# Weight operands of the first feed-forward projection off their 32-byte edges

## The chip, the cores and the metric

The kernel runs on one core of a Trainium2 chip. The metric is the device time of one execution in microseconds (us), the median over the runs.

## The reference

One layer of an encoder over 2048 tokens with 1024 features, in float32: windowed attention (16 query heads, 4 key and value heads, 128 tokens to each side, a bias by distance and a learned sink), then a SwiGLU feed-forward network with 2816 hidden features. Each sub-layer has a norm before and after it and is scaled, shifted and gated by a vector c. The part that the change touches is the first projection of the feed-forward network:

```python
def swiglu(h, w_in, w_out):
    a, b = jnp.split(h @ w_in, 2, axis=-1)
    return (jax.nn.silu(a) * b) @ w_out
...
        h = rmsnorm(x, ffn_norm_pre[i]) * (1.0 + sc2) + sh2
        y = swiglu(h, ffn_w_in[i], ffn_w_out[i])
        x = x + g2 * rmsnorm(y, ffn_norm_post[i])
```

## The kernel before

**Stages.** The tokens go in four chunks of 512. The projections to queries, keys and values, the attention in blocks of 128 queries, and the output projection (tiles `ol` and `wo`) come first and are interleaved; they fill some 700 us. Then come the two feed-forward projections, each in two halves of 1024 tokens.

**Precision.** Every float32 operand is held as two tiles of a rounded type: a high part, made by a cast on ScalarE, and a low part, the difference of value and high part, made by a subtraction on VectorE (`split`). A product takes three matmuls (`three`): high by high, high by low, low by high. The first factor of each is the stationary one, which TensorE loads (LDWEIGHTS) before each matmul; the second one streams through in 512 columns.

**The feed-forward projections.** A `Block` is a product of 2 by 2 blocks by Strassen's method in Winograd's form: seven products in place of eight. It loads two column tiles of weights (`wiri`), makes four sums and differences of their quarters on VectorE (`s1` to `s4`), and splits seven operands `a11`, `s2`, `a12`, `s3`, `s1`, `a22`, `s4` into tiles `w...` of 2 by 4 by 128 words a partition: the high part, then the low part, each with four stationary operands of 128 by 128. In the profile they are named `wa_i` and `ws_i`. Each of the seven products takes 4 times 3 matmuls, and `Hidden.take` adds the results up on VectorE (`p1`, `u2`, `u3`, `b1` as `p_i`, `u_i`, `b_i`); the moving operands are `hb` and `ht`. There are 22 blocks for each half of the tokens. Products of the two halves of SwiGLU and the differences for the second projection are written for GpSimd.

**Places.** The operand tiles of the first projection come from two pools, `wi0` and `wi1`, used in turn by the blocks, each with a tag `w` of 7 places. The second projection (`Outs`) uses the same `Block` with a pool `wo` of 11 places. A place's size is rounded up to 32 bytes, and places stand one behind the other from an address that is a multiple of 32; other tiles of the stage lie behind them in the same memory.

**Order.** A recording layer takes down all operations, gives each tile a place and each engine its order, and only then emits the program, so every instruction has the line of the emitting call (L748). Priorities come from a backward pass, and of 18 rounds the one with the best replay is kept. The planner knows which rows and which pieces of 64 words of a tile an operation touches (`Buf.unit`, `region`), and which earlier tiles lay where a new one comes to lie (`place`). An addition or product that the kernel writes for GpSimd may be given to VectorE (`others`). Transfers are all issued from one queue (SyncE).

One line elsewhere has a part in the prediction: the probabilities of the attention, which are transposed as stationary operands:

```python
            pr = pp.tile([P, GRP, 3 * P + 1], F32, tag="pr", name=f"pr{u}")
...
                    pe.transpose(pt[:, h * P:(h + 1) * P], pr[:, h, jj * P:(jj + 1) * P], ident)
```

With P = 128 and GRP = 4, a head's row is 385 words. The other transposes, of values (`vt`), take blocks of 128 words from rows of 512.

Of the kernel before, what the change touches and what calls it, by code (L numbers as in the profile page):

```python
# [14 lines left out]
F32R = mybir.dt.float32r  # L15
# [5 lines left out]
P = 128  # L21
# [731 lines left out]
def f(ap):  # L753
    return ap.bitcast(F32)
# [8 lines left out]
def encoder_layer(ctx, tc, a):  # L763
# [81 lines left out]
    def split(hi, lo, src, eng):  # L845
        act.copy(hi, src)
        return eng.tensor_tensor(lo, src, f(hi), ALU.subtract)
# [8 lines left out]
    class Chunk:  # L856


        def __init__(self, c):
            self.c, self.hh = c, [None] * KT  # L860
            self.xt = [xs.tile([P, CH], F32, tag="x", name=f"x{c}_{k}") for k in range(KT)]
            for k in range(KT):
                sp.dma_start(self.xt[k], a["xT"][c, :, k, :])
# [524 lines left out]
    wbufs = 7  # L1388
# [6 lines left out]
    class Operands:  # L1395
# [12 lines left out]
        def load(self, *names):  # L1408

            for n in names:  # L1410
                for k in range(self.m):
                    hi, lo = self.slot(n, k)
                    sp.dma_start(f(lo), self.src(n, k))
                    split(hi, lo, f(lo), dve)

    class Block:

        STEPS = tuple(zip(("a11", "s2", "a12", "s3", "s1", "a22", "s4"), OPERANDS))

        def __init__(self, ops, i, u, wa, wb, keep=None, kept=None):  # L1420
            self.ops, self.u, m = ops, u, ops.m
            pl = wi[i % len(wi)]
            if kept:
                self.w = {}
                for n, _ in self.STEPS:
                    self.w[n] = w = pl.tile([P, 2, m, P], F32R, tag="w", bufs=wbufs, name=f"w{n}_{u}")
                    sp.dma_start(f(w), kept[n])
                return
            raw = pl.tile([P, 2, 2 * m, P], F32, tag="raw", name=f"wir{u}")
            sp.dma_start(raw[:, 0], wa)  # L1430
            sp.dma_start(raw[:, 1], wb)
            a11, a12, a21, a22 = [raw[:, i].rearrange("p (k e) c -> p e k c", e=2)[:, e] for i in range(2) for e in range(2)]
            sm_ = {n: pl.tile([P, m, P], F32, tag=n, name=f"{n}_{u}", bufs=1) for n in ("s1", "s2", "s4")}
            sm_["s3"] = a21
            dve.tensor_tensor(sm_["s1"], a21, a22, ALU.add)
            dve.tensor_tensor(sm_["s2"], sm_["s1"], a11, ALU.subtract)
            dve.tensor_tensor(sm_["s3"], a11, a21, ALU.subtract)
            dve.tensor_tensor(sm_["s4"], a12, sm_["s2"], ALU.subtract)
            src = dict(sm_, a11=a11, a12=a12, a22=a22)
            self.w = {}  # L1440
            for n, _ in self.STEPS:
                w = pl.tile([P, 2, m, P], F32R, tag="w", bufs=wbufs, name=f"w{n}_{u}")
                split(w[:, 0], w[:, 1], src[n], dve)
                self.w[n] = w
                if keep:
                    sp.dma_start(keep[n], f(w))
# [155 lines left out]
    wbufs = 11  # L1602
# [120 lines left out]
    t0, m = 2 * FIRST[-1][-1], 2 * PARTS[-1][-1]  # L1723
    gs, wl = {}, []
    for j in range(CPH):
        c = NCH - CPH + j
# [4 lines left out]
    for n in range(KT):  # L1731
        raw = wi[0].tile([P, 2, 2 * MD * P], F32, tag="raw", name=f"wlr{n}").rearrange("p a b -> p (a b)")[:, :m * P]
        sp.dma_start(raw, a["w_out"][n, :, t0:t0 + m].rearrange("p k c -> p (k c)"))
        t = hB.tile([P, 2, CH], F32R, tag=("t1", "t4", "b22")[n // 3], name=f"wl{n}")
# [3 lines left out]
    for i, (c, cols) in enumerate([(NCH - 2, slice(0, CH)), (NCH - 1, slice(0, CH // 2)), (NCH - 1, slice(CH // 2, CH))]):  # L1738
        for n in range(KT):
# [4 lines left out]
            for k in range(m):  # L1744
                w, g = wl[n], gs[c, k]
# [83 lines left out]
```

## Time and profile before

| | |
|---|---|
| median of the runs | 2037.47 us |
| runs | 2036.68 to 2038.26 us (2) |
| profiled execution, its own time | 2036.67 us |
| its span, first to last instruction | 2034.9 us |
| mean granted TensorE clock | 0.995 |

PE is TensorE's matmuls, PEld its weight loads, DVE VectorE, ACT ScalarE, POOL GpSimd, SP the queue that issues transfers. A tile's buffer numbers are left out of its name, so that `ws_i` stands for all operands of the first projection made from a sum or difference. In `bank<-ht,ws_i` the moving operand stands first and the stationary one second. Where durations are given as three numbers, they are the least, the median and the greatest, in ns. What an engine waited for is inferred from semaphores.

### The profile page before, as it was taken

How to read it: one execution, taken by the hardware profiler on the slowest of the kernel's cores; microseconds unless marked ns; L12 is line 12 of the kernel's file. 1: busy time of each engine (PE TensorE's matmuls, PEld its weight loads, DVE VectorE, ACT ScalarE, POOL GpSimd, SP SyncE). 2: the span in 40 equal slices, each digit the busy share in tenths (PEclk: the TensorE clock that was granted, in tenths of full speed). 3: DMA queues.
4: the chain of work that ended last, by engine and by line, in shares of the span. 5: the costliest groups of instructions: out<-in, count | busy, mean ns of one | idle time of the engine just before them, and what ended most of it. 6: DMA issues, size and time to landing. Idle time of an engine off the chain costs nothing.

```text
span 2034.9 us, 28945 instructions
## 1 busy us (share of the span) xinstructions
PE 1991.0 (98%) x9366; PEld 1659.3 (82%) x9366; DVE 1703.6 (84%) x3075; ACT 1069.9 (53%) x2094; POOL 554.4 (27%) x501
## 2 busy tenths in 40 slices
PE   5999999999999999999999999999999999999997
PEld 4888888888787778788888888888888888888886
DVE  7868888877989888988787998776776789989998
ACT  5557766777778864344343533333333744455432
POOL 1302342344657513432333221111111000120031
PEclk9999999999999999999999999999999999999999
DMA  8896765576787694444446743333233694398543
GB/s 308 303 324 211 241 210 173 192 279 229 253 279 251 226 361 150 160 161 166 165 160 242 272 155 130 119 135 104 83 124 105 240 334 144 117 326 297 173 154 109
DMA packets 208580, 415.23 MB, mean 204 GB/s; under 512 B 19963, under 2 KB 61996, under 8 KB 205356
## 3 DMA queue, kind: packets, MB, share of 16 engines
q1 hardware_dynamic: 207852, 412.84, 58.7%
q8 instruction: 75, 1.23, 0.2%
q14 instruction: 77, 0.63, 0.1%
q10 hardware_dynamic: 576, 0.52, 0.1%
HBM read 278.52 MB, written 134.77 MB: 203 GB/s over the span
## 4 chain that ended last, share of the span: by engine, by line
PE 91%; DVE 5%; DMA 2%; issue 1%; ACT 1%; SPq 0%; POOL 0%; DVEq 0%; ACTq 0%; POOLq 0%
PE bank L748 91%; DVE z L748 1%; DVE ada L748 1%; DVE zx L748 1%; DVE pr L748 0%; DMA o_d<-of 0%; DMA ly<-y_d 0%; DMA x<-xT 0%; DMA ol<-o_d 0%; SPq L748 0%; DVE u_i L748 0%; DMA ada<-ada_w 0%; DVE x L748 0%; DVE plo L748 0%; DVE ws_i L748 0%
## 5 line engine op out<-in xcount | busy, mean ns | idle before, releaser
L748 PE MATMUL bank<-ht,ws_i 128*128 128x512 f32 x1584 | 374.0, 389 | 0.0
L748 PEld LDWEIGHTS bank<-ht,ws_i 128*128 128x128 f32 x1584 | 297.3, 188 | 61.7
L748 PE MATMUL bank<-hb,wa_i 128*128 128x512 f32 x1056 | 254.2, 389 | 0.4 <-DVE hb L748 0.4
L748 PEld LDWEIGHTS bank<-hb,wa_i 128*128 128x128 f32 x1056 | 198.1, 188 | 42.0 <-DVE hb L748 0.7
L748 PE MATMUL bank<-ol,wo 128*128 128x512 f32 x768 | 206.1, 396 | 2.3 <-ACT yacc L748 1.1
L748 DVE TENSOR_TENSOR u_i<-bank,u_i 128x512 f32<-128x512 f32 x176 | 120.9, 688 | 80.0 <-PE bank L748 77.8
L748 ACT CAST ws_i<-s_i 128x512 fp32r<-128x512 f32 x132 | 81.9, 620 | 192.2 <-DVE s_i L748 96.2
L748 ACT ACTIVATE pr<-pr,nm 128x385 f32<-128x385 f32 (+1 forms) x256 | 154.8, 606 | 53.3 <-DVE nm L748 47.4
L748 DVE CUSTOM_DVE_ANT_0 pr<-bank,bias,nsink 128x384 f32<-128x384 f32 (+1 forms) x256 | 149.9, 594 | 25.6 <-PE bank L748 22.0
L748 PEld LDWEIGHTS bank<-ol,wo 128*128 128x128 f32 x768 | 141.2, 188 | 28.7 <-ACT yacc L748 1.5
L748 POOL TENSOR_SCALAR pr<-pr,rs 128x384 f32<-128x384 f32 (+1 forms) x177 | 114.7, 660 | 179.7 <-DVE rs L748 168.3
L748 POOL TENSOR_TENSOR p_i<-p_i,u_i 128x512 f32<-128x512 f32 x41 | 66.9, 1632 | 344.6 <-DVE u_i L748 173.9
L748 POOL TENSOR_TENSOR z<-z,z 128x512 f32<-128x512 f32 x29 | 45.4, 1577 | 345.9 <-ACT ws_o L748 264.4
L748 PE MATMUL bank<-k,q 128*128 128x384 f32 (+1 forms) x512 | 135.5, 345 | 1.5 <-DVE nm L748 1.5
L748 PE MATMUL bank<-hi,ws 128*128 128x512 f32 x384 | 134.3, 400 | 0.0
L748 DVE TENSOR_TENSOR plo<-bank,phi 128x512 fp32r<-128x512 f32 x184 | 120.8, 684 | 9.8 <-ACT phi L748 8.7
L748 PE MATMUL bank<-hb,ws_i 128*128 128x512 f32 x528 | 127.1, 390 | 1.8 <-ACT p_i L748 1.8
L748 ACT CAST wa_i<-wiri 128x512 fp32r<-128x512 f32 x132 | 81.3, 620 | 90.1 <-PE bank L748 78.4
L748 PE MATMUL bank<-ht,wa_i 128*128 128x512 f32 x528 | 126.8, 389 | 0.0
L748 DVE TENSOR_TENSOR wa_i<-wiri,wa_i 128x512 fp32r<-128x512 f32 x132 | 103.4, 784 | 19.0 <-ACT wa_i L748 19.0
L748 PEld LDWEIGHTS bank<-hb,ws_i 128*128 128x128 f32 x528 | 98.9, 188 | 23.2 <-ACT p_i L748 2.6
L748 DVE TENSOR_TENSOR z<-bank,z 128x512 f32<-128x512 f32 (+1 forms) x164 | 107.7, 659 | 11.4 <-PE bank L748 10.2
(261 smaller groups left out, 4422.6 us busy)
## 6 DMA issues: line engine op xcount, KB each, us to landing
wiri<-w_in SPq DMA_DIRECT2D x88, 512.0 KB, 4.6
ada<-ada_w SPq DMA_DIRECT2D x40, 512.0 KB, 5.1
q_d<-e SPq DMA_DIRECT2D x32, 512.0 KB, 4.4
q<-q_d SPq DMA_DIRECT2D x16, 1024.0 KB, 7.0
wo<-wo_d SPq DMA_DIRECT2D x16, 1024.0 KB, 6.0
wiro<-w_out SPq DMA_DIRECT2D x40, 384.0 KB, 5.0
g_d_b<-p_i SPq DMA_DIRECT2D x44, 256.0 KB, 3.3
g_d_t<-p_i SPq DMA_DIRECT2D x40, 256.0 KB, 2.0
```

Of the source, the lines that this page charges most:

```text
L748: o.ins = getattr(engs[o.eng], o.fn)(*args, **kw)
```

## The change

A new function `operand` makes the operand tiles of a `Block`. For the second projection (pools whose name begins with `wo`) it does what was done before. For the first it makes a tile of 8 words more, and gives out a view of it that begins 0 to 7 words (0 to 28 bytes) behind its start, one word further for each tile that is made, and round again after eight. The places stand 4128 bytes apart, 4096 before.

```diff
+    shift = iter(range(1 << 20))
+
+    def operand(pl, m, name):
+        if pl.name[:2] == "wo":
+            return pl.tile([P, 2, m, P], F32R, tag="w", bufs=wbufs, name=name)
+        t = pl.tile([P, 2 * m * P + 8], F32R, tag="w", bufs=wbufs, name=name)
+        i = next(shift) % 8
+        return t[:, i:i + 2 * m * P].rearrange("p (a k c) -> p a k c", a=2, c=P)
+
     class Block:
...
                 for n, _ in self.STEPS:
-                    self.w[n] = w = pl.tile([P, 2, m, P], F32R, tag="w", bufs=wbufs, name=f"w{n}_{u}")
+                    self.w[n] = w = operand(pl, m, f"w{n}_{u}")
                     sp.dma_start(f(w), kept[n])
...
             for n, _ in self.STEPS:
-                w = pl.tile([P, 2, m, P], F32R, tag="w", bufs=wbufs, name=f"w{n}_{u}")
+                w = operand(pl, m, f"w{n}_{u}")
                 split(w[:, 0], w[:, 1], src[n], dve)
```

Kinds and numbers of operations stay as they were, but the planner gives them in part another order and another engine. Up to the last two units of the attention all engines' orders are the same. There TensorE's order begins to differ; `ident,pr` are transposes of probabilities, `k,q` the scores, `ol,wo` the output projection of the third chunk. Before:

```order
L748 MATMUL bank<-ident,pr_3_6896 128x128 x4
L748 MATMUL bank<-k_3_6468,q_3_6460 128x256
L748 MATMUL bank<-ident,pr_3_6896 128x128 x4
L748 MATMUL bank<-k_3_6468,q_3_6460 128x256
L748 MATMUL bank<-ol_1_5218,wo_5_6769 128x512 x3
L748 MATMUL bank<-ol_2_6043,wo_5_6769 128x512 x2
L748 MATMUL bank<-k_3_6468,q_3_6460 128x256 x2
```

and now:

```order
L748 MATMUL bank<-ident,pr_3_6896 128x128 x8
L748 MATMUL bank<-k_3_6468,q_3_6460 128x256 x2
L748 MATMUL bank<-ol_1_5218,wo_5_6769 128x512 x3
L748 MATMUL bank<-ol_2_6043,wo_5_6769 128x512 x3
L748 MATMUL bank<-k_3_6468,q_3_6460 128x256 x2
```

One score matmul stands behind all eight transposes in place of between them, and one more matmul of the output projection stands ahead of the next scores. Differences of this kind go on to the second block of the first projection; later TensorE's order is the same but for the banks that it writes and for one exchange near the end of the first projection.

The second place is GpSimd in the first half of the first projection. Rows `p_i<-p_i,u_i` and `u_i<-u_i,b_i` are SwiGLU's products, `lacc` the sum of squares of a late norm, `ly` and `lh` its scaling, the others differences for the second projection. Before:

```order
L748 TENSOR_TENSOR p_i_14_9986<-p_i_14_9986,u_i_14_10017 128x512
L748 TENSOR_TENSOR u_i_14_10002<-u_i_14_10002,b_i_14_10032 128x512
L748 TENSOR_TENSOR lacc_9612<-lacc_9612,xsq_6_10100 128x512
L748 TENSOR_TENSOR p_i_14_9986<-u_i_14_10002,p_i_14_9986 128x512
L748 TENSOR_TENSOR p_i_15_10147<-p_i_15_10147,u_i_15_10173 128x512
L748 TENSOR_TENSOR u_i_15_10154<-u_i_15_10154,p_i_14_9986 128x512
L748 TENSOR_TENSOR lh_0_10348<-lh_0_10348,lr_10247 128x512
```

and now:

```order
L748 TENSOR_TENSOR lacc_9633<-lacc_9633,xsq_6_10075 128x512
L748 TENSOR_TENSOR ly_7_10079<-ly_7_10079,lr_9490 128x512
L748 TENSOR_TENSOR u_i_14_9992<-u_i_14_9992,b_i_14_10059 128x512
L748 TENSOR_TENSOR p_i_14_9986<-u_i_14_9992,p_i_14_9986 128x512
L748 TENSOR_TENSOR lh_0_10371<-lh_0_10371,lr_10264 128x512
```

Of this stretch's operations one product of block 14, a product of block 15 and a difference have gone to VectorE, and one scaling has come. Over the program GpSimd has 506 instructions before and 485 now, VectorE 3077 and 3098: 21 have moved. TensorE, ScalarE and the transfer queue have as many as before.

## The prediction

> **What bounds the kernel now.** I read the page's summary first, then the chain of waits, then the busy time of each engine by stretch, and last the instructions of single tiles. From the page:
>
> ```profile
> span 2034.9 us, 28945 instructions
> PE 1991.0 (98%) x9366; PEld 1659.3 (82%) x9366; DVE 1703.6 (84%) x3075; ACT 1069.9 (53%) x2094; POOL 554.4 (27%) x501
> PE 91%; DVE 5%; DMA 2%; issue 1%; ACT 1%; SPq 0%; POOL 0%; DVEq 0%; ACTq 0%; POOLq 0%
> ```
>
> TensorE's matmuls fill 98% of the span and 91% of the chain that ends last. A busy TensorE says little alone, so I look at where the chain leaves it. One piece of the chain, in order of time (start, length, what):
>
> ```profile
> 842.92 1157.88 PE bank L748 x5124
> ```
>
> For 1157.88 us nothing but matmuls follow each other. By stretches:
>
> ```profile
> core 0: us, PE busy (x) PEld busy (x) DVE busy (x) ACT busy (x) POOL busy (x), PEclk, DMA share, GB/s
> 678.00:716.00 38.00, 35.56 (x170) 28.14 (x169) 30.29 (x53) 31.23 (x56) 19.22 (x17) 1.00 0.87 306
> 716.00:800.00 84.00, 83.72 (x369) 69.31 (x370) 70.12 (x98) 49.47 (x82) 20.00 (x14) 1.00 0.71 254
> 800.00:843.00 43.00, 41.21 (x182) 33.48 (x180) 39.34 (x46) 13.14 (x23) 22.01 (x15) 1.00 0.53 181
> 1150.00:1200.00 50.00, 50.00 (x222) 41.42 (x221) 49.19 (x75) 25.70 (x45) 13.88 (x8) 1.00 0.62 222
> 1200.00:1600.00 400.00, 400.00 (x1767) 331.20 (x1766) 299.68 (x479) 142.13 (x246) 64.86 (x42) 1.00 0.36 123
> 716.00:1600.00 884.00, 881.92 (x3888) 729.53 (x3889) 719.18 (x1060) 356.81 (x604) 222.56 (x145) 1.00 0.47 165
> ```
>
> The first feed-forward projection runs from about 716 to 1600 us. TensorE is busy for 881.92 of its 884 us at the full granted clock, one matmul every 400/1767 = 226.4 ns. There is nothing to win in this stage except at its entrance (0.28 us to 800 and 1.79 us from 800 to 843) and in the last of the attention ahead of it (2.44 us from 678 to 716). What can be lost is cover: VectorE has 884 − 719.18 = 165 us left over the stage, but only 0.81 us between 1150 and 1200.
>
> **The change part by part.** The first part is the weight loads. The tile view of the weight operands (duration ns min/median/max, first and last start):
>
> ```profile
> L748 PEld LDWEIGHTS bank<-ht,ws_i x1584: 187/188/188, 750.2 to 1583.8; 128*128 128x128 f32 x198
> L748 PEld LDWEIGHTS bank<-hb,ws_i x528: 186/188/189, 763.8 to 1589.3; 128*128 128x128 f32 x176
> L748 PEld LDWEIGHTS bank<-hb,wa_i x1056: 186/188/189, 708.2 to 1578.4; 128*128 128x128 f32 x176
> L748 PEld LDWEIGHTS bank<-ht,wa_i x528: 187/188/188, 761.1 to 1588.6; 128*128 128x128 f32 x176
> L748 ACT CAST ws_i<-s_i x132: 603/622/627, 703.6 to 1551.8; 128x512 fp32r<-128x512 f32 x132
> L748 DVE TENSOR_TENSOR ws_i<-s_i,ws_i x132: 674/684/1789, 713.8 to 1552.5; 128x512 fp32r<-128x512 f32 x132
> ```
>
> These are 1584 + 528 + 1056 + 528 = 3696 loads of 44 blocks with 7 operands each, 12 loads an operand. The offset goes round 0 to 7 words over the 308 operands, so 39 stay on the edge and 269 leave it: 3228 loads read from an address 4 to 28 bytes off. Their cover: a load takes 188 ns and the next begins 226 ns after it, so about (400 − 331.20)/1766 = 39 ns of each period are idle on the load side. An off-edge load costs nothing until it is 39 ns longer.
>
> Does it get longer? The kernel already loads off-edge operands. In the attention each probability tile `pr` has rows of 3·128 + 1 = 385 words a head, 1540 bytes, which is 48 times 32 and 4 over; head h begins 4h bytes past an edge, so three of four transposes load their stationary operand 4, 8 or 12 bytes off. The value transposes load from `vt`, whose blocks of 512 bytes are all on the edge. The same form of instruction, side by side:
>
> ```profile
> L748 PEld LDWEIGHTS bank<-ident,pr x736: 137/140/231, 174.4 to 689.9; 128*128 128x128 f32 x184
> L748 PEld LDWEIGHTS bank<-ident,vt x16: 137/140/143, 217.0 to 250.3; 128*128 128x128 f32 x16
> ```
>
> Minimum and median are equal, 137 and 140 ns, with 552 of the 736 off the edge; a cost of being off would stand in that median. These are transposes at 140 ns and not loads of the rounded type at 188 ns, and they show no offset from 16 to 28 bytes, so I keep a price for the case that this doesn't carry over (below). Even then there is more cover than 39 ns: near the end, matmuls of 256 columns follow each other with loads of the same rounded type.
>
> ```profile
> L748 PEld LDWEIGHTS bank<-gls,wl x288: 186/192/193, 1972.0 to 2018.5; 128*128 128x128 f32 x144
> 1998.07 17.03 PE L748 MATMUL bank<-gls,wl 128*128 128x256 f32 x135
> ```
>
> 135 matmuls in 17.03 us are one every 126 ns, with a load of 192 ns each. Loads thus overlap, and one can be fed every 126 ns, where this stage asks for one every 226. I take 0 for the loads; the bounds are 0 and the doubled load of the third rival.
>
> [...]
>
> The second part is the making of the operands: 269 of 308 casts on ScalarE and as many subtractions on VectorE write, and the subtractions also read, off the edge. Nearest rows, again with three of four off:
>
> ```profile
> L748 DVE CUSTOM_DVE_ANT_0 pr<-bank,bias,nsink x256: 454/609/621, 162.9 to 684.3; 128x384 f32<-128x384 f32 x112, 128x256 f32<-128x256 f32 x16
> L748 ACT ACTIVATE pr<-pr,nm x256: 494/618/642, 163.6 to 685.5; 128x385 f32<-128x385 f32 x112, 128x257 f32<-128x257 f32 x16
> ```
>
> The same by shape, with the mean of the full-width form behind the comma (160 to 690 us):
>
> ```profile
> L748 ACT ACTIVATE pr<-pr,nm 128x385 f32<-128x385 f32 x224 | 138.7, 619 | 51.1 <-DVE nm L748 45.3 <-POOL pr L748 3.9 <-DVE rs L748 1.2
> L748 DVE CUSTOM_DVE_ANT_0 pr<-bank,bias,nsink 128x384 f32<-128x384 f32 x224 | 135.1, 610 | 18.7 <-PE bank L748 15.3 <-POOL pr L748 1.8
> ```
>
> If being off were dear, three quarters would be long and one short, and the mean would lie well under the greatest. VectorE's mean is 610 against 621, so the quarter on the edge can't be shorter than 610 − 3 · 11 = 577 ns; on ScalarE it is 619 − 3 · 23 = 550. That leaves 44 and 92 ns at the most, and the equal heads are the simpler reading. I take 0. The upper end is 269 · 44 ns = 12 us more on VectorE, under its 165 us of idle time, and 269 · 92 ns = 25 us on ScalarE, which idles for 884 − 357 = 527 us. Tiles behind the weights in their pools move too, the moving operands among them; if each of 3696 streams took 1 ns more, the resolution of these rows, it would be 3.7 us. I take 0 there as well.
>
> The third part is the order. It is the same up to the last two units of the attention, where the trace stands at 678 us, and from the third block of the first projection on TensorE's order differs in bank names and at one place near 1600 us. Between these the matmuls are regrouped; over the whole projection, 21 additions and products go from GpSimd to VectorE. Their two prices:
>
> ```profile
> L748 DVE TENSOR_TENSOR p_i<-p_i,u_i x23: 678/686/1800, 807.4 to 1607.5; 128x512 f32<-128x512 f32 x23
> L748 POOL TENSOR_TENSOR p_i<-p_i,u_i x41: 1292/1631/2793, 769.6 to 1590.8; 128x512 f32<-128x512 f32 x41
> ```
>
> VectorE gets 21 · 0.69 = 14.5 us more work, which the 165 us of idle time cover if it comes where the idle time is. TensorE's waits in the reordered part add up to 2.44 + 0.28 + 1.79 = 4.5 us; that is all that a better order could take away. Upwards the bound is the 14.5 us, should all of it come where VectorE is full, and 12 us more with the bound for its off-edge writes. I take +1 us, since a new order has 4.5 us of short waits to shift about, and no reason to be much better or worse.
>
> The sum, on the profiled execution's own 2036.67 us (its span is 2034.9): 0 + 0 + 0 + 1 = 2037.7 us. That execution lies 0.8 us under the median of the runs, 2037.47, so the forecast is **2038.5 us**, within 2034 to 2043 if this is the case that holds.
>
> **The rivals.**
>
> First, VectorE falls behind: the 14.5 us come where it is full, from 800 to 843 or around 1150 us, subtractions for the next block end late, and TensorE waits at a block's first matmul. For it: 39.34 busy of 43 us and 49.19 of 50 there. Against it: from 1200 on VectorE is idle for a quarter, and two sets of operand places let it work a block ahead. Time: 2037.5 + 14.5 = 2052 us.
>
> Second, the new order closes the waits before 843 us: 2037.5 − 4.5 = 2033. For it, the waits are there to be closed. Against it, the chain goes into the 2.44 us of them through two transfers, the last attention output to memory and back for the output projection, which an order of matmuls doesn't shorten:
>
> ```profile
> 695.38 7.74 DMA o_d<-of
> 703.13 7.07 DMA ol<-o_d
> ```
>
> Third, the other side: off-edge loads of the rounded type run longer, and longer than their cover. It decides from 39 ns on, if a load must end before its matmul begins: each further ns costs 3228 · 0.001 = 3.2 us, 2% (41 us) is reached at 39 + 13 = 52 ns, and a doubled load, 188 ns more, costs 149 ns · 3228 = 481 us, that is 2519 us. For it: no row of this profile has a load of that type off the edge. Against it: the equal `pr` and `vt` rows, and the 126 ns spacing, by which a load could grow by 100 ns unseen.
>
> That the change is without effect on the addresses is no rival: the tiles have 8 words more and every view starts at its own offset.
>
> **How the numbers follow.** The forecast has 0.77, the first rival 0.10, the second 0.06, the third 0.06 (0.05 of it beyond 2%), and 0.01 stays for a gain that I see no place for. The range from 2030 to 2053 us holds the forecast and the first two rivals; the third is left out. About 2% is what a measurement of this kernel can tell from no change: faster by that 0.01, within it 0.94, slower 0.05.
>
> **What would show it.** Right: LDWEIGHTS of `wa_i` and `ws_i` again at 186 to 189 ns, matmuls of that stage 226 ns apart, casts at 622 and subtractions at 684 ns in the median, the unbroken matmul piece from about 843 to 2000 us still there, VectorE some 15 us busier and GpSimd some 30 us less. Wrong: a load's median above 188, a spacing above 227 ns in 716 to 1600, or waits of TensorE for `ws_i`, `wa_i` or `u_i` of VectorE near 1150 us. A cost of offsets alone would show as a second, larger duration in seven of eight operands.

## The result and the profile after

The changed kernel takes 2057.74 us (median of 2057.44 and 2058.05) against 2037.47: the ratio is 1.0103, with a 95% interval from 1.0086 to 1.0119. That is within the 2% that were forecast as likeliest, but 4.7 us above the upper end of the range, 2053 us, and 19.2 us above the forecast. The profiled execution has a span of 2056.2 us, 21.3 us more than before. The prediction's number was wrong, and so was the reason behind it.

The page of the changed kernel, span and busy times:

```profile
span 2056.2 us, 28876 instructions
PE 2012.7 (98%) x9366; PEld 1661.3 (81%) x9366; DVE 1704.3 (83%) x3096; ACT 1075.1 (52%) x2094; POOL 525.3 (26%) x480
```

TensorE's busy time grew by 2012.7 − 1991.0 = 21.7 us, the whole loss; its idle time is what it was (43.5 us, 43.9 before). So TensorE waits no longer than before; its matmuls take longer. The chain of waits has the stage as one piece of matmuls again, up to its end at 1610 us (start, length, what):

```profile
718.39 891.55 PE bank L748 x3842
```

891.55 us for 3842 matmuls is 232.1 ns for one; before, the long piece had 1157.88/5124 = 226.0. The same by stretches, with the columns of the prediction's table:

```profile
678.00:716.00 38.00, 33.92 (x152) 26.51 (x151) 33.93 (x55) 26.80 (x48) 14.93 (x13) 0.93 0.84 303
716.00:800.00 84.00, 83.67 (x361) 67.94 (x360) 69.58 (x92) 49.97 (x82) 20.77 (x14) 0.99 0.70 252
800.00:843.00 43.00, 43.00 (x188) 34.97 (x187) 36.66 (x52) 16.22 (x28) 19.73 (x13) 1.00 0.53 179
1200.00:1600.00 400.00, 400.00 (x1724) 323.63 (x1723) 280.43 (x446) 128.47 (x216) 64.80 (x42) 1.00 0.32 111
1650.00:1750.00 100.00, 100.00 (x442) 82.78 (x442) 90.63 (x164) 45.07 (x88) 0.00 (x0) 1.00 0.68 239
```

From 1200 to 1600 us TensorE is busy for all 400 us, at the full granted clock, as before; but 1724 matmuls fit in and not 1767, one every 232.0 ns and not 226.4. In the second projection (1650 to 1750) it is 442 in 100 us, 226.2 ns, and 443 before:

```profile
1650.00:1750.00 100.00, 100.00 (x443) 82.81 (x442) 89.58 (x161) 45.63 (x85) 0.00 (x0) 1.00 0.61 207
```

The loss is a longer distance in time from one matmul's start to the next, in the first projection only. Read from the starts of all its matmuls (without the few pauses over 300 ns) the mean is 226.68 ns before and 232.18 after: 5.50 ns · 3696 = 20.3 us.

The weight loads, which the prediction watched, look as if nothing had happened (least, median, greatest):

```profile
L748 PEld LDWEIGHTS bank<-ht,ws_i x1584: 187/188/194, 753.0 to 1607.9; 128*128 128x128 f32 x198
L748 PEld LDWEIGHTS bank<-hb,ws_i x528: 187/188/192, 767.0 to 1609.3; 128*128 128x128 f32 x176
L748 ACT CAST ws_i<-s_i x132: 603/622/625, 697.5 to 1571.8; 128x512 fp32r<-128x512 f32 x132
L748 DVE TENSOR_TENSOR ws_i<-s_i,ws_i x132: 675/687/1786, 709.4 to 1572.5; 128x512 fp32r<-128x512 f32 x132
```

The timeline of TensorE near 1000 us (start, time to the modelled end of the last, the group) shows where the time goes, one row for the 12 matmuls of one product:

```profile
999.73 2.88 PE L748 MATMUL bank<-ht,wa_i 128*128 128x512 f32 x12
1002.45 2.97 PE L748 MATMUL bank<-hb,ws_i 128*128 128x512 f32 x12
1005.26 2.96 PE L748 MATMUL bank<-hb,wa_i 128*128 128x512 f32 x12
1008.06 2.26 PE L748 MATMUL bank<-ht,ws_i 128*128 128x512 f32 x9
```

From start to start the first takes 2.72 us (12 · 226.7 ns), the second 2.81 (234 ns), the third 2.80 (233 ns). The weights of the first begin 36 bytes past a 64-byte edge and it runs at the old pace. Whatever costs the time is a matter of the single product, and being off an edge is not enough for it.

In the addresses (read here and below from the places that the emitted program gives its operands, with its matmuls taken in the order of the trace) two things had changed: the weights begin 0 to 28 bytes into places of 4128 bytes, and the pools have grown by 7 · 32 = 224 bytes each, which moved all tiles behind them, so that every moving operand of the stage lies 32 bytes off a 64-byte edge. Before, all operands of TensorE in this stage, moving and stationary, began on multiples of 512 bytes.

### The profile page after: what moved, and what is told of

The parts are those of the page before. It is cut to its first block, busy times and chain, and to the rows that moved or that the text cites. A ratio compares the mean times of both kernels' runs of the same rounds, so it can differ in the third digit from the quotient of the medians.

```text
span 2056.2 us, 28876 instructions
## 1 busy us (share of the span) xinstructions
PE 2012.7 (98%) x9366; PEld 1661.3 (81%) x9366; DVE 1704.3 (83%) x3096; ACT 1075.1 (52%) x2094; POOL 525.3 (26%) x480
## 4 chain that ended last, share of the span: by engine, by line
PE 89%; DVE 5%; DMA 3%; ACT 1%; issue 1%; POOL 0%; SPq 0%; DVEq 0%; ACTq 0%; POOLq 0%
PE bank L748 89%; DVE ada L748 1%; DVE z L748 1%; DVE pr L748 1%; DVE zx L748 0%; DMA hb<-h_d 0%; DVE plo L748 0%; DMA wsr<-w_qkv 0%; DMA wor<-w_o 0%; DVE lo L748 0%; DMA wqkv<-w_qkv 0%; DVE x L748 0%; DMA y_d<-y 0%; DVE of L748 0%; DMA ol<-o_d 0%
## 5 line engine op out<-in xcount | busy, mean ns | idle before, releaser
L748 PE MATMUL bank<-ht,ws_i 128*128 128x512 f32 x1584 | 382.2, 394 | 0.0
L748 PE MATMUL bank<-hb,wa_i 128*128 128x512 f32 x1056 | 260.7, 395 | 0.0
L748 POOL TENSOR_TENSOR p_i<-p_i,u_i 128x512 f32<-128x512 f32 x32 | 51.3, 1604 | 323.5 <-DVE u_i L748 176.6
L748 PEld LDWEIGHTS bank<-ht,wa_i 128*128 128x128 f32 x528 | 99.4, 188 | 23.1
```

What stands on the lines that cost most here:

```text
L748: o.ins = getattr(engs[o.eng], o.fn)(*args, **kw)
```

## The experiments

All times are medians, with ratios against runs of the kernel before on the same chip (medians of 2035.6 to 2037.0 us). Behind most runs stands the row for 1200 to 1600 us, to be compared with x1767 before and x1724 after; where the offsets differ from product to product, spacings by operand or distance stand instead. A spacing is the mean time from one matmul's start to the next, without pauses over 300 ns.

**Which operand is it? Four runs.** First the offsets alone, with the moving operands back on a 64-byte edge.

```diff
-        t = pl.tile([P, 2 * m * P + 8], F32R, tag="w", bufs=wbufs, name=name)
+        t = pl.tile([P, 2 * m * P + 16], F32R, tag="w", bufs=wbufs, name=name)
```

> The offsets of the weight operands stay (0 to 28 bytes, one after the other), but their places stand 64 bytes further apart in place of 32, so that each pool grows by 448 bytes and all tiles behind it, the moving operands hb and ht among them, lie on a 64-byte edge again, as before the change. Theory M (what costs is the moving operand, which the change put 32 bytes off a 64-byte edge): spacing of the first projection's matmuls 226.7 ns again, time about 2038 us (2034 to 2042). Theory S (what costs is the weight operand off its edge): spacing about 232 ns, time about 2058 us. Theory P (the distance between the places, so where the weights lie against each other): open, some value between.

Measured: 2058.59 us, ratio 1.0107 (1.0091 to 1.0124).

```profile
1200.00:1600.00 400.00, 400.00 (x1723) 323.61 (x1723) 281.88 (x449) 127.26 (x214) 64.78 (x42) 1.00 0.32 110
```

Theory M falls in its simple form: no moving operand is off a 64-byte edge, and the loss is all there. Products whose weights have the offset 0 are slow as well (230.9 ns in the mean), which S does not explain.

Then the wide places alone.

```diff
-        i = next(shift) % 8
+        i = 0
```

> The places stand 32 bytes further apart as in the change, but every weight operand starts at the edge of its place: no offsets. All moving operands still lie 32 bytes off a 64-byte edge, and half of the weights too. Theory M: spacing 232 ns, about 2058 us (2054 to 2062). Theory S: spacing 226.7 ns, about 2038 us. Theory P: as M.

Measured: 2060.86 us, ratio 1.0121 (1.0106 to 1.0136).

```profile
1200.00:1600.00 400.00, 400.00 (x1722) 322.93 (x1721) 281.42 (x449) 127.35 (x214) 64.83 (x42) 1.00 0.31 110
```

The offsets, which the change is named after, are not needed for the loss: 32 bytes between the places cost the same. Theory S falls.

Then the kernel before, with nothing but two unused tiles:

```diff
     hA = open_pool(early, "hA", KT // 2)
+    hA.tile([P, 8], F32, tag="gap", name="gap0", bufs=1)
...
     wi[1] = open_pool(ffn, "wi1", side="right")
+    wi[1].tile([P, 8], F32, tag="gap", name="gap1", bufs=1)
```

> The kernel before, weights and their places untouched, with one unused tile of 32 bytes ahead of the moving operands in each of two pools, so that hb and ht lie 32 bytes off a 64-byte edge while every weight operand lies on one. Theory M: 3696 matmuls at about 232 ns, about 2058 us (2054 to 2062). Theories S and P: 226.7 ns and about 2038 us.

Measured: 2067.95 us, ratio 1.0153 (1.0138 to 1.0169), and 233.32 ns in the mean.

```profile
1200.00:1600.00 400.00, 400.00 (x1716) 321.48 (x1715) 284.05 (x452) 127.16 (x214) 64.89 (x42) 1.00 0.32 109
```

Theories S and P fall here, for neither the weights nor their places have moved. The spacing alone makes (233.32 − 226.68) · 3696 = 24.5 us. Of the other 7 us some 5 lie ahead of the stage, where the planner chose another order: the first load for `hb,wa_i` starts at 713.3 us, 708.2 before.

```profile
L748 PEld LDWEIGHTS bank<-hb,wa_i x1056: 186/187/330, 713.3 to 1608.4; 128*128 128x128 f32 x176
```

The fourth was meant to give the edge that matters: eight offsets for the places of four moving operands, in places 64 bytes further apart.

```diff
+            if pl.name in ("hA", "hB"):
+                t = pl.tile([P, 2 * CH + 16], F32R, tag=n, name=f"h{n}{self.u}_{k}")
+                i = (0, 1, 2, 4, 8, 12, 15, 0)[2 * k + (n in ("t2", "b22"))]
+                t = t[:, i:i + 2 * CH].rearrange("p (a c) -> p a c", a=2)
```

> The kernel before, with the moving operands b11, t2, b22 and t4 alone moved, each of their eight places by its own offset: 0, 4, 8, 16, 32, 48, 60 and 0 bytes from a 64-byte edge. The other three operands stay on their edge. To be read from the trace by offset. Theory M: about 232 ns for every offset but 0 if each stream that straddles one more 64-byte line pays, only for 32 and more if it is something else; 1584 of 3696 matmuls are off, so about 2037 + 1584 x 5.6 ns = 2046 us. Theories S and P: 226.7 ns for all, about 2038 us.

Measured: 2050.87 us, ratio 1.0073 (1.0058 to 1.0088). No order by offset comes out: 4 bytes off gives 236.2 ns, 32 gives 231.1, 60 gives 230.3. But the rows with offset 0 were not free either. Since the places stand 64 bytes further apart, they lie 128, 320 and 448 bytes past a multiple of 512, and take 232.0, 234.4 and 232.9 ns. Of the three operands that stayed on multiples of 512 bytes, t3 and t1 run at 226.7 ns; b21, whose products come behind those of t2, has slow matmuls among its first six and 226.7 ns from then on. So 64 bytes was the wrong unit.

**Edge or distance? Three runs.** Each operand's own edge of 64 or 512 bytes, or the distance of moving and stationary operand from each other (theory R): in the kernel before both are kept. First one distance for each moving operand, by gap tiles between them:

```diff
+    def gap(pl, size, name):
+        pl.tile([P, size // 4], F32, tag=name, name=name, bufs=1)
+
+    gaps = dict(t2=32, b21=32, t3=64, t1=128, b22=32)
     wi = [open_pool(early, "wi0"), None]
...
     wi[1] = open_pool(ffn, "wi1", side="right")
+    gap(wi[1], 96, "gapw")
...
+            if n in gaps:
+                gap(pl, gaps.pop(n), f"gap{n}")
```

> Weights as in the kernel before, each on a 512-byte edge; unused gap tiles put each moving operand, with all of its four tiles, at one distance past a 512-byte edge: b11 0, t2 32, b21 64, t3 128, t1 256, t4 384, b22 416. Read by operand from the trace. Theory 64 (a stream that starts off a 64-byte edge pays one 16-column beat more, 6.67 ns): t2 and b22 at 233 ns, the others at 226.7, time 2037 + 1056 x 6.67 ns = 2044 us. Theory 512 (only the 512-byte edge is free): all but b11 at 233 ns, 2037 + 3168 x 6.67 ns = 2058 us. Between them an edge of 128 or 256 bytes would leave t3, t1 and t4, or t1 alone, at 226.7 ns. Theory R (only the distance between moving operand and weights counts): here the same as theory 512.

Measured: 2054.43 us, ratio 1.0090 (1.0075 to 1.0105). By operand, past a 512-byte edge: t2 (32) 233.5 ns, b21 (64) 229.9, t3 (128) 231.8, t1 (256) 227.3, t4 (384) 232.6, b22 (416) 233.6. The timeline near 1000 us shows four in a row, t4, b22, b11 of the next block, t2:

```profile
999.96 2.95 PE L748 MATMUL bank<-ht,wa_i 128*128 128x512 f32 x12
1002.75 2.97 PE L748 MATMUL bank<-hb,ws_i 128*128 128x512 f32 x12
1005.56 2.91 PE L748 MATMUL bank<-hb,wa_i 128*128 128x512 f32 x12
1008.30 2.97 PE L748 MATMUL bank<-ht,ws_i 128*128 128x512 f32 x12
1011.10 2.92 PE L748 MATMUL bank<-hb,wa_i 128*128 128x512 f32 x12
```

From start to start they take 2.79, 2.81, 2.74 and 2.80 us: b11, on the edge, is the short one, though above its 2.72: its first six matmuls, behind slow ones, are slow in part, the others are about 227 ns apart. Theory 64 falls with t3 and t4. 256 bytes are nearly free, 128 are not. (The 6.67 ns of the expectations stand beside a measured 233.32 − 226.68 = 6.64 ns, from the run with the moving operands 32 bytes on and the kernel before. In the last piece of the trace of before, `gls` by `wl`, 512 columns come every 226.7 ns and 256 every 120, 0.417 ns a column, so 6.67 ns are 16 columns by estimate; that a stream pays by beats of 16 was the author's supposition and is shown by no run.)

The same with the weights moved instead:

```diff
+        t = pl.tile([P, 2 * m * P + 16], F32R, tag="w", bufs=wbufs, name=name)
+        return t[:, :2 * m * P].rearrange("p (a k c) -> p a k c", a=2, c=P)
...
+    gap(hA, 64, "gapa")
...
+    gap(wi[1], 64, "gapw")
```

> The moving operands on a 512-byte edge, all of them; the seven places of the weights stand 64 bytes further apart, without offsets, so they lie 0, 64, 128, 192, 256, 320 and 384 bytes past a 512-byte edge (in the second pool the same in another order). Theory 64: no operand is off an edge, 226.7 ns everywhere, 2037 us. Theory 512: about 233 ns wherever the weights are not at 0, 2037 + 3168 x 6.67 ns = 2058 us. Theory R: as theory 512. A theory by which the moving operand alone counts: 2037 us.

Measured: 2053.26 us, ratio 1.0085 (1.0070 to 1.0100), below the 2058 us of theory 512. With the weights 64 bytes on: 233.0 ns; 128: 232.6; 192: 229.6; 256: 227.7; 320: 233.3; 384: 231.7. Theory 64 falls again, and with it the moving operand alone. Beside the run before, both fit one function of the distance, moving less weights, modulo 256: weights 64 or 320 bytes on are distance 192, with 233.0 and 233.3 ns; 192 on is distance 64, with 229.6, and the moving operand 64 on is the same distance, with 229.9.

Last, everything moved together:

```diff
     wi = [open_pool(early, "wi0"), None]
+    gap(wi[0], 32, "gap0")
...
+    gap(open_pool(ffn, "wi1g", side="right"), 480, "gap1")
     wi[1] = open_pool(ffn, "wi1", side="right")
```

> Weights and moving operands of the first projection all 32 bytes past a 512-byte edge, so that their distance from each other is that of the kernel before. Theory R: 226.7 ns, about 2037 us. Theories 64 and 512 (each stream for itself): 233 ns, 2037 + 3696 x 6.67 ns = 2062 us.

Measured: 2042.26 us, ratio 1.0031 (1.0018 to 1.0043).

```profile
1200.00:1600.00 400.00, 400.00 (x1765) 331.16 (x1765) 289.93 (x463) 136.69 (x233) 64.77 (x42) 1.00 0.35 120
```

226.71 ns in the mean, the old spacing, with every operand 32 bytes off. Edges are out, the distance it is. Of the 6 us that remain, the spans show 4.1 (2039.0 and 2034.9): TensorE is busy 2.7 us longer (1993.7) and idle 1.4 us longer. The spacing in the stage is the old one, so they come from elsewhere; the order is another, but whether it costs them was not tried.

**A forecast from the distance. Five runs.** If the distance modulo 256 decides, a time can be told from addresses alone. To have room for any distance, the places became 256 bytes wider, for which two of ten temporary tiles were given up. Only one number differs between three kernels: `i` is 39 for distance 100, 41 for distance 92 and 0 for distance 0.

```diff
+        t = pl.tile([P, 2 * m * P + 64], F32R, tag="w", bufs=wbufs, name=name)
+        i = 39
+        return t[:, i:i + 2 * m * P].rearrange("p (a k c) -> p a k c", a=2, c=P)
...
-    tmp = open_pool(ffn, "tmp", 10, side="right")
+    tmp = open_pool(ffn, "tmp", 8, side="right")
```

> All moving operands of the first projection on a 256-byte edge; every weight operand 156 bytes past one (the places are 256 bytes wider, and two of ten temporary tiles are given up to make room), so the distance, moving less weights, is 100 bytes modulo 256 everywhere. In the changed kernel and with its places 64 bytes apart, the passes that happened to have this distance ran at 226.7 ns. Theory R256 (the distance modulo 256 decides, whatever edge is missed): 226.7 ns throughout, within 3 us of the control with distance 0. Theory E (a weight operand off a 64-byte edge costs a beat): 233 ns, 25 us above the control.

> The same with the weight operands 164 bytes past the 256-byte edge, 8 bytes further: distance 92. In the changed kernel the passes with this distance had a mean of 237.3 ns. Theory R256: about 237 ns throughout, 3696 x 10.6 ns = 39 us above the control. Theory E: 233 ns, 25 us above the control and equal to the run with 156 bytes.

> The control of these two: the same wide places and eight temporary tiles, but weight operands at the edge of their places, distance 0 modulo 256. Both theories: 226.7 ns. The time is that of the kernel before, about 2037 us, plus what the two temporary tiles and the other order cost, 0 to 10 us.

Measured: distance 100: 2037.87 us, ratio 1.0002 (0.9993 to 1.0012); distance 92: 2076.25, 1.0197 (1.0182 to 1.0213); the control: 2038.09, 1.0008 (0.9998 to 1.0018). The long piece of the chain of waits, first distance 100, then 92:

```profile
717.84 1281.02 PE bank L748 x5657
```

```profile
717.82 1320.12 PE bank L748 x5657
```

The same 5657 matmuls without a gap take 39.10 us longer; 39 were expected. The two rows from 1200 to 1600 us, in the same order:

```profile
1200.00:1600.00 400.00, 400.00 (x1766) 331.15 (x1765) 299.03 (x475) 138.27 (x237) 48.89 (x33) 1.00 0.34 119
```

```profile
1200.00:1600.00 400.00, 400.00 (x1687) 318.69 (x1686) 288.40 (x454) 126.40 (x210) 49.11 (x33) 1.00 0.31 108
```

With all weights 156 bytes past a 256-byte edge, 28 off the nearest 64-byte edge below, the kernel is as fast as before; 8 bytes further it loses 38 us. Theory E falls in both runs.

The second projection, by gaps of 32 and 480 bytes ahead of its moving operands:

```diff
     hA = open_pool(ctx, "hA2", MD)
+    hA.tile([P, 8], F32, tag="gapa", name="gapa", bufs=1)
...
+    open_pool(ctx, "hB2g", side="right").tile([P, 120], F32, tag="gapb", name="gapb", bufs=1)
     hB = b21p = t3p = open_pool(ctx, "hB2", MD, side="right")
```

> The kernel before, with an unused tile of 32 and one of 480 bytes ahead of the second feed-forward projection's moving operands, so that they lie 32 bytes past a 256-byte edge and its weights on one; the first projection is left alone. The 288 matmuls of the last piece (gls by wl) have both operands moved by the same 32 bytes. Theory R256: the 1680 matmuls of the second projection at about 233 ns, those of the last piece unchanged; time 2037 + 1680 x 6.6 ns = 2048 us. If the effect belonged to the first projection's surroundings alone: 2037 us.

Measured: 2047.17 us, ratio 1.0053 (1.0038 to 1.0068).

```profile
1200.00:1600.00 400.00, 400.00 (x1765) 330.97 (x1764) 301.32 (x478) 140.30 (x242) 64.88 (x42) 1.00 0.36 124
1650.00:1750.00 100.00, 100.00 (x430) 80.33 (x429) 89.11 (x158) 44.90 (x86) 0.00 (x0) 1.00 0.63 211
```

Now the first projection keeps its pace and the second has 430 matmuls in 100 us where there were 443, 232.6 ns each; the starts give 233.32, the very number of the first projection at distance 32. The last piece, with both operands moved, stays at 226.67 for its matmuls of 512 columns. The effect belongs to the addresses, not to the stage.

Last, all 64 distances in one run (against the changed kernel):

```diff
-        t = pl.tile([P, 2 * m * P + 8], F32R, tag="w", bufs=wbufs, name=name)
-        i = next(shift) % 8
+        t = pl.tile([P, 2 * m * P + 64], F32R, tag="w", bufs=wbufs, name=name)
+        i = next(shift) % 64
...
-    tmp = open_pool(ffn, "tmp", 10, side="right")
+    tmp = open_pool(ffn, "tmp", 8, side="right")
```

> As the control with distance 0 (wide places, eight temporary tiles), but each weight operand starts 4 bytes further into its place than the one before, 0 to 252 bytes and round again: all 64 distances in one run. Theory R256, with the means of the changed kernel's passes by distance (56 distances, mean 232.3 ns): the spacing of each distance is the same as there, about 226.7 ns at 0, 28, 100 and 136, 230 to 237 at most others, and the whole 2038 + 3696 x 5.6 ns = 2059 us. If the distance modulo 256 were not all that decides (modulo 512, or what ran before), some distances differ from there by more than 3 ns, at 188 and 228 first, where two runs already disagree.

Measured: 2058.97 us, ratio 1.0115 (1.0098 to 1.0132). The 2059 us of the expectation were worked out from the changed kernel's products one distance at a time. By distance (bytes, moving less weights, modulo 256; mean ns from start to start, without the first two of a product):

```
distance        0     28     64     92    100    136    152    160    172    176    192    224
changed         -    226.7  229.2  237.3  226.7  226.9  233.3  234.7  234.7  232.1  232.9  232.6
all distances 227.7  226.7  230.0  237.3  226.7  226.7  233.1  234.6  235.3  232.0  233.4  232.7

distance        4     40    112    124    132    140    156    228
changed       233.4  231.1  233.4  227.6  233.3  230.6  230.1  226.7
all distances 226.7  232.2  226.7  230.7  231.8  233.4  227.3  235.3
```

The changed kernel has 48 of the 64 distances (the expectation has 56), and 0 is not among them. Of these 48, 40 agree within 1 ns. The second table is the other eight, and part of the expectation missed there: 228 was named as doubtful, 188 agreed, and seven others were not foreseen. Modulo 512 explains none of them: the new run has both halves of each, which lie under 0.4 ns apart for seven of the eight and 1.1 ns apart for 156. For these eight the distance is not all.

The kept traces show what else has a part: the product that comes just ahead. In the changed kernel there are five products at distance 40, all with the same two addresses. Four of them come behind a product at distance 236 and take 232.2 or 232.3 ns; the fifth comes behind one at 164 and takes 226.7. At distance 124 it is 226.6 or 226.7 ns behind distance 160 (four products) and 231.7 behind distance 4 (one, slow in its first eight spacings and then at 226.7). In the run with all distances, 156 takes 226.6 or 226.7 ns behind 160 (four) and 230.0 behind 184 (one). For all eight distances the two kernels have other products ahead. So the pace of a product goes by its own distance and, at some distances, by how it begins. This is read off the traces; no run changed the product ahead alone.

Of the 64 distances 6 are below 227.5 ns (4, 28, 100, 112, 136 and 156), 31 between 232.5 and 234, and 7 above. Distance 0, here behind products at distance 4, stands at 227.7.

No run beats the kernel before: with all its distances 0 it is already at the lowest spacing that any run showed.

## Why the prediction was wrong

**The weight loads (taken as 0).** Their recorded time is what was forecast, 188 ns in the median and 194 at the most. But whether a load outgrows its 39 ns of cover was the wrong question. The loss stands in the time from one matmul's start to the next, and the loads' own rows show none of it. The 126 ns spacing of `gls,wl`, read as room to spare, was measured with both operands at distance 0.

**The `pr` and `vt` rows.** They are true and did not carry over. They compare durations of loads that run beside transposes of 128 columns, never the spacing of 512-column matmuls beside a weight operand at another distance. In the stage itself the trace of before holds distance 0 alone, so it could not price the change; that was a reason for a wider range upwards.

**The step that failed** is the one on the neighbours: "if each of 3696 streams took 1 ns more, the resolution of these rows, it would be 3.7 us. I take 0 there as well." The place was right, 3696 streams one after another with nothing to hide them, and the size was not: 5.50 ns, 20.3 us. One nanosecond was the resolution of a row and no bound. Nor was it the neighbours' own new place that cost the time: with the moving operands back on 64-byte edges the loss stayed (2058.59 us). What costs is the distance between moving operand and weights, which moving either one changes, and the prediction had no term for it. With it fell the forecast spacing of 226 ns. That spacing was named as what would show the prediction wrong ("a spacing above 227 ns in 716 to 1600"), and it did.

**The third rival** had the right sign and the wrong mechanism. It asked for loads longer than their cover, in the 3228 off the edge, at 3.2 us for each ns. No load grew, products off the edge run at the old pace at distances 28, 100 and 136, and products on it are slow (400/1722 = 232.3 ns in the run with wide places alone).

**The operands' making** cost nothing, as forecast: casts at 622 ns, subtractions at 687 against 684.

**The order** (taken as +1 us, bounds −4.5 and +14.5) cost nothing that can be seen. TensorE's waits from 678 to 843 us are 4.08 + 0.33 + 0 = 4.4 us, 4.5 before, only placed otherwise. GpSimd has 29 us less to do, as forecast. VectorE has not the 15 us more: 1704.3 us and 1703.6. It has 157 instructions above 1 us, 183 before, so its other work became shorter as GpSimd's fell; whether one is the cause of the other was not tried. The first two rivals, both on the order, did not come about: `wa_i` and `ws_i` are not waited for at 1150 us.

## What to carry to other kernels

Where matmuls follow each other without a gap, compare start to start, not the durations of the weight loads alone: here a loss of 2.4% (226.68 to 232.18 ns) left them at 188 ns in the median. Whoever pads or shifts a tile moves all tiles behind it; work out the distance, modulo 256 bytes, of each moving operand from the weights that go with it, before and after, and keep it at 0 when in doubt. Products in a row should all have it: behind products at other distances the first matmuls at distance 0 were slow too (2.74 us for the twelve of b11 in the run by operand, 2.72 where all are at 0). A harmless-looking gap of 32 bytes costs here more than the whole change did (24.5 us of spacing against 20.3), and a trace in which a distance never occurs says nothing about its price.

## What the runs showed of the hardware

- A matmul of 512 columns with its own weight load is repeated every 226.7 ns at distance 0, whether both operands lie on a 512-byte multiple (226.68, the kernel before) or 32 bytes off it (226.71). At most other distances it is 230 to 235 ns in the changed kernel and the run with all distances, with a crowd at 233.3, which is 6.6 ns more; the most was 237.3, at 92 bytes.
- The spacing within a product isn't even. In the changed kernel's five products at distance 92 the matmuls are 229 to 257 ns apart one by one, in a pattern that repeats (230, 229, 234, 257 and 237 ns in the first). At some distances the pace also depends on the product just ahead: at distance 40, with the same addresses, it was 232.2 ns behind distance 236 and 226.7 behind 164.
- Why the distance counts is not shown: no run here took the weight load or the stream away. What 8 bytes of it are worth is measured: 2037.87 us at distance 100 and 2076.25 at 92, 38.4 us apart.
- No edge of the weights alone decides it. With every weight operand on a multiple of 64 bytes (the run with the weights moved by steps) the spacing still rose to 233.3 ns, at 320 bytes; with every one 156 bytes past a multiple of 256 (distance 100) 1766 matmuls fit in 400 us, 226.5 ns each, where the kernel before has 1767.
